# Expert stage in a fixed order, and neighborhood attention in 4 by 16 patches

## The chip, the cores and the metric

The kernel runs on one core of one Trainium2 chip. The metric is the time of one execution in microseconds of device time. The time before is the median of three runs; the profile is one execution taken by the hardware profiler.

## The reference

One encoder block on a sequence of 1024 tokens (16 rows of 64 columns) of width 1024, in float32:

```python
h = rms_norm(x, norm_mix_g)
(na_q, na_k, na_v, p_r, p_k, p_v, lat_w, lat_a, lat_g, mem_q, gates) = split_columns(h @ w_in)
y_na  = neighborhood_attention(na_q, na_k, na_v, na_rpb)      # 6 heads of 64
y_rw  = rwkv7_bidirectional(...)                              # 6 heads, two directions
y_mem = memory_attention(mem_q, rms_norm(mem), w_mem_kv)      # 4 heads, 256 memory rows
x = x + (sum of sigmoid(gate_b) * (y_b @ w_branch_b)) @ w_out
x = x + expert_choice_ffn(rms_norm(x), w_router, w_gate, w_up, w_down)
return rms_norm(x, norm_final_g)
```

Two parts matter here. In neighborhood attention the token at row r, column c sees 8 rows and 16 columns: the rows start at clip(r - 4, 0, 8), the columns at clip(c - 8, 0, 48), and each pair gets a bias `rpb[head, row offset, column offset]` before the softmax. In the expert stage each of 16 experts takes the 128 tokens with the highest affinity, and computes `silu(x Wg) * (x Wu)` (1024 to 2048) times `Wd` (2048 to 1024), scaled by the affinity and added to the tokens' rows.

## The kernel before

Every product in reduced precision is made from three: an operand is split into a hi part (rounded by a ScalarE copy) and a lo part (the rest, by a VectorE subtraction), and hi x hi, lo x hi and hi x lo are accumulated (`mm3`, lines 220 to 223).

The work goes by stages: input norms and projections; the RWKV scan with the other projections as filler; neighborhood attention, group norm and memory attention together; merge of the branches; output projection, router and top-k; experts; final norm. SP issues most loads and stores, in the order of its queue.

**Attention stage.** Head pairs j = 0, 1, 2 have 16 items each, one for a row r of 64 queries of two heads (128 partitions of scores), then 16 items of memory attention. `na_load(j)` loads k (`kt`), q, v (`VC`) and the bias table, splits k and q (`KT`, `qb`; q is masked per head), adds the column mask to the bias on GpSimd, and turns v into `VT` by 15 transposes, with one ScalarE copy for four of them. `na_item(j, r)` has eight parts: `score` (three matmuls of 512 key columns: 8 rows of 64, then bias and row maximum in one VectorE operation), `exp` (ScalarE), `recip` and `mul` (VectorE), `trans` (four transposes and a ScalarE copy), `mix` (value product, for four blocks of keys and two heads), `hi` and `lo` (result to `yh`, `yl`). The order is written out by hand: at slot n each part runs for the item that its lag in `PIPE` gives (score 0, exp 1, recip and mul 2, trans 3, mix 5, hi and lo 6). `na_load(0)` stands ahead of all items; `na_load(1)`, `na_load(2)` and `mem_load` begin at slots 1, 17 and 33, and group norm, one part per slot, at slot 5. Group norm loads its own data through SP and applies a tanh to `lg` on ScalarE at slot 6. Of `VC` and `kt` there is one buffer each.

**Expert stage.** The weights lie in 384 tiles of 1 MB, each loaded by SP into one of 14 buffers (`raw`, `RAWB`), and split by ScalarE into `ewh` (line 1212) and by VectorE into `ewl` (line 1213), of which there are four buffers each (`SPLB`). A step is one expert e and one block f of 512 of the 2048 hidden columns: two gate tiles (24 matmuls), the down part of the step before (24), two up tiles (24). The down part transposes the activation `sg` (line 1277), splits it into `ah` and `al` (lines 217 and 218) and multiplies by two down tiles (lines 1285 to 1287). `load_x` gathers an expert's 128 rows (line 1254), transposes and splits them; after an expert, `ye` is scaled and scattered with addition into `acc` (line 1292). The order of this stage is left to the framework's planner. At the end all rows of `acc` are normalised (line 1322) and stored while the last down part runs, and the last expert's rows are gathered, completed (line 1336), normalised and scattered over the stored ones.

Of the kernel before, what the change touches and what calls it, by code (L numbers as in the profile page):

```python
# [25 lines left out]
F32 = mybir.dt.float32  # L26
# [37 lines left out]
def shape_constants():  # L64
# [42 lines left out]
def lay(inputs):  # L107
# [36 lines left out]
    return {k: np.ascontiguousarray(v) for k, v in o.items()}  # L144


@with_exitstack
def block_kernel(ctx: ExitStack, tc: tile.TileContext, T, out, dbg=None, upto=99):
# [668 lines left out]
    def na_load(j):  # L817
        bias = ap.tile([128, 15, 64], F32, name="bias", bufs=2)
        q = ap.tile([128, S], F32, name="q", bufs=2)
        kt = ap.tile([128, S], F32, name="kt", bufs=1)  # L820
        VC = ap.tile([128, S], F32, name="VC", bufs=1)
        for t, src in ((kt, pna[3 + j]), (q, pna[j]), (VC, pna[6 + j]), (bias.rearrange("p r c -> p (r c)"), T["rpb"][:, j])):
            SP.dma_start(t, src)
        VT = ap.tile([128, 15, 128], F32, name="VT", bufs=2)
        qb = [ap.tile([128, 16, 2, 64], F32R, name=f"qb{v}", bufs=2) for v in "hl"]
# [7 lines left out]
        q = q.rearrange("p (r t) -> p r t", t=64)  # L833
        for h, r in ((0, 0), (1, 0), (0, 8), (1, 8)):
            hi, lo = (v[:, r:r + 8, h] for v in qb)
            V.tensor_scalar(hi, q[:, r:r + 8], C("hsel")[:, h:h + 1], None, op0=OP.mult)
            yield
            V.scalar_tensor_tensor(lo, q[:, r:r + 8], C("hsel")[:, h:h + 1], hi.bitcast(F32), op0=OP.mult, op1=OP.subtract)
            if r:
                yield  # L840
        G.tensor_tensor(bias, bias, C("nmask")[:, None, :].to_broadcast([128, 15, 64]), op=OP.add)
        for i0 in range(0, 15, 4):
            p = abank("tr")
            n = min(4, 15 - i0)
            for i in range(i0, i0 + n):
                t0 = i * 128 if i < 8 else (i - 8) * 128 + 64
                PE.transpose(p[:, (i - i0) * 128:(i - i0 + 1) * 128], VC[:, t0:t0 + 128], ident)
            A.activation(VT[:, i0:i0 + n], p[:, :n * 128].rearrange("p (i c) -> p i c", i=n), AF.Copy)
            yield

    def na_item(j, r):
        bias, KT, qb, VT = na[j]
        rs = min(max(r - 4, 0), 8)
        ro = rs - r + 7
        o = {}

        def score():
            s = abank("s")
            mm3(s, 0, 1, *(v[:, r].rearrange("p h t -> p (h t)") for v in qb), *(v[:, rs * 64:rs * 64 + 512] for v in KT))
            o["sb"] = sb = ap.tile([128, 512], F32, name="sb", bufs=4)  # L860
            o["st"] = st = ap.tile([128, 8], F32, name="st", bufs=4)
            V.tensor_tensor_reduce(out=sb, in0=s, in1=bias[:, ro:ro + 8, :].rearrange("p r c -> p (r c)"),
# [12 lines left out]
        def trans():  # L875
            p = abank("tr")
            for k in range(4):
                PE.transpose(p[:, k * 128:(k + 1) * 128], o["sb"][:, k * 128:(k + 1) * 128], ident)
            o["pt"] = ap.tile([128, 512], F32, name="pt", bufs=3)
            A.activation(o["pt"], p, AF.Copy)  # L880
# [486 lines left out]
```

## Time and profile before

| | |
|---|---|
| median of three runs | 2420.95 us (2419.74 to 2422.48) |
| profiled execution, first to last instruction | 2419.1 us |
| matmul queue (PE) busy | 2279.5 us, 94% |
| VectorE (DVE) busy | 1725.5 us, 71% |
| ScalarE (ACT) busy | 1334.0 us, 55% |
| GpSimd (POOL) busy | 592.8 us, 25% |
| moved by DMA | 588.55 MB, 243 GB/s in the mean |
| attention stage, about 823 to 999 us | 176 us |
| expert stage with the end, about 1250 to 2419 us | 1169 us |

How to read the lines: a row of the timeline is start in us, duration in us, engine, line of the kernel, instruction, the tile it writes and the tiles it reads, count, and in brackets the idle time of the engine before it with what ended it. PE is the matmul, PEld the weight load. A row of a stretch gives its length, then the busy time of PE, PEld, DVE, ACT and POOL with their instruction counts, the granted TensorE clock as a share of full speed, the busy share of the 16 DMA engines, and GB/s. A row of a group gives its busy time, the mean duration in ns, and idle time before. A row of the chain is start and duration of one piece. A row of the waits is who waited for whom: us in all, times, longest. Matmuls are pipelined, so starts tell their pace, not their durations.

### The profile page before, as it was taken

To read this page: it belongs to the slowest core of one execution; us is meant where nothing else is said; L and a number is where in the kernel's file an instruction comes from. 1 tells how busy PE (TensorE), PEld (TensorE's weight loads), DVE (VectorE), ACT (ScalarE), POOL (GpSimd) and SP (SyncE) were. 2 spreads that over 40 slices of the span, in tenths; PEclk is the share of its full clock that TensorE was granted. 3 is DMA by queue.
4 is the path that set the end of the run, shared out by engine and by line. 5 is a ranking of instruction groups with operands and counts; after the bars stand their busy time and mean duration, and the time that the engine had idled before them with its cause. 6 is when DMAs were issued, how large, how long until landed. Compare 5 with 4: busy or idle time off the path is not lost.

```text
span 2419.1 us, 34315 instructions
## 1 busy us (share of the span) xinstructions
PE 2279.5 (94%) x12931; PEld 1819.1 (75%) x12931; DVE 1725.5 (71%) x2155; ACT 1334.0 (55%) x1616; POOL 592.8 (25%) x1187
## 2 busy tenths in 40 slices
PE   7999999999999989999939999999999999999997
PEld 6677788877778767778727777777777777777775
DVE  6556556655665488762378888888888888888887
ACT  6554333333343378522236776776767667767675
POOL 1000666766666243340140000000011101011001
PEclk9999999999999999999969999999999999999998
DMA  6435443444343331363769999999999999999894
GB/s 233 151 137 209 129 122 98 117 126 125 98 119 96 122 111 64 116 191 121 250 267 372 357 367 364 355 360 375 362 370 362 361 359 374 365 375 367 295 413 173
DMA packets 193910, 588.55 MB, mean 243 GB/s; under 512 B 53072, under 2 KB 97360, under 8 KB 144592
## 3 DMA queue, kind: packets, MB, share of 16 engines
q1 hardware_dynamic: 187120, 562.88, 64.0%
q0 software_dynamic: 4752, 17.30, 2.8%
q10 hardware_dynamic: 1872, 6.17, 0.7%
q8 instruction: 102, 1.67, 0.3%
q14 instruction: 64, 0.52, 0.1%
HBM read 517.56 MB, written 68.73 MB: 242 GB/s over the span
## 4 chain that ended last, share of the span: by engine, by line
PE 64%; DVE 21%; issue 5%; ACT 4%; DMA 2%; POOL 2%; SPq 0%; POOLq 0%; DVEq 0%; ACTq 0%
PE acc L695 12%; DVE ewl L1213 8%; PE u L223 5%; PE y L1286 4%; PE y L1285 4%; PE y L1287 4%; PE u L221 3%; PE u L222 3%; PE acc L221 3%; PE acc L223 3%; PE acc L222 3%; PE g L221 3%; PE g L223 3%; PE g L222 3%; ACT ewh L1212 2%
## 5 line engine op out<-in xcount | busy, mean ns | idle before, releaser
L1213 DVE TENSOR_TENSOR ewl<-raw,ewh 128x2048 fp32r<-128x2048 f32 x380 | 861.7, 2289 | 162.0 <-ACT ewh L1212 161.8
L1212 ACT ACTIVATE ewh<-raw 128x2048 fp32r<-128x2048 f32 x384 | 732.2, 1917 | 289.0 <-PE y L1286 149.4
L223 PE MATMUL u<-ewl,xh 128*128 128x512 f32 x512 | 206.3, 403 | 23.8 <-DVE ewl L1213 22.0
L1292 POOL DMA_INDIRECT acc<-ye,idx x15 | 40.0, 2666 | 768.3 <-DVE ye L1291 768.3
L695 PE MATMUL acc<-hlo,wh 128*128 128x512 f32 x560 | 225.6, 403 | 0.0
L695 PE MATMUL acc<-hhi,wh 128*128 128x512 f32 x560 | 225.1, 402 | 0.0
L695 PE MATMUL acc<-hhi,wl 128*128 128x512 f32 x560 | 225.0, 402 | 0.0
L551 POOL TENSOR_TENSOR tmul<-tinv,blk 96x60 f32<-96x60 f32 (+24 forms) x496 | 172.1, 347 | 151.8 <-DMA blk<-ldr 114.3
L221 PE MATMUL u<-ewh,xh 128*128 128x512 f32 x512 | 205.5, 401 | 0.0
L1285 PE MATMUL y<-ewh,ah 128*128 128x512 f32 x512 | 194.7, 401 | 8.6 <-ACT ah L217 8.6
L221 PE MATMUL g<-ewh,xh 128*128 128x512 f32 x512 | 201.2, 393 | 0.0
L1286 PE MATMUL y<-ewh,al 128*128 128x512 f32 x512 | 200.4, 391 | 0.8 <-DVE al L218 0.8
L1287 PE MATMUL y<-ewl,ah 128*128 128x512 f32 x512 | 199.9, 390 | 0.0
L222 PE MATMUL u<-ewh,xl 128*128 128x512 f32 x512 | 199.9, 390 | 0.0
L223 PE MATMUL g<-ewl,xh 128*128 128x512 f32 x512 | 199.9, 390 | 0.0
L222 PE MATMUL g<-ewh,xl 128*128 128x512 f32 x512 | 199.5, 390 | 0.0
L553 POOL TENSOR_TENSOR tinv<-tinv,tmul 96x60 f32<-96x60 f32 (+24 forms) x496 | 176.2, 355 | 38.9
L223 PEld LDWEIGHTS u<-ewl,xh 128*128 128x128 f32 x512 | 96.0, 188 | 67.2 <-DVE ewl L1213 49.5
L1285 PEld LDWEIGHTS y<-ewh,ah 128*128 128x128 f32 x512 | 92.4, 189 | 42.3 <-ACT ah L217 23.7
L218 DVE TENSOR_TENSOR wl<-wraw,wh 128x1024 fp32r<-128x1024 f32 (+1 forms) x60 | 76.1, 1269 | 65.1 <-ACT wh L217 65.0
L695 PEld LDWEIGHTS acc<-hlo,wh 128*128 128x128 f32 x560 | 106.2, 190 | 20.6
L695 PEld LDWEIGHTS acc<-hhi,wl 128*128 128x128 f32 x560 | 105.9, 189 | 20.2
(309 smaller groups left out, 4409.4 us busy)
## 6 DMA issues: line engine op xcount, KB each, us to landing
raw<-in_wg_dram SPq DMA_DIRECT2D x128, 1024.0 KB
raw<-in_wu_dram SPq DMA_DIRECT2D x128, 1024.0 KB
raw<-in_wd_dram SPq DMA_DIRECT2D x128, 1024.0 KB
wraw<-in_wt_dram SPq DMA_DIRECT2D x46, 512.0 KB
pt<-pz SPq DMA_DIRECT2D x16, 768.0 KB
pgt<-po SPq DMA_DIRECT2D x48, 256.0 KB
gt<-pgt SPq DMA_DIRECT2D x16, 768.0 KB
blk<-ldr SPq DMA_DIRECT2D x64, 96.0 KB
```

The costliest lines, as they stand in the source:

```text
L218: V.tensor_sub(lo, src, hi.bitcast(F32))
L221: PE.matmul(out_, lh, rh, start=(k_ == 0), stop=False)
L222: PE.matmul(out_, ll, rh, start=False, stop=False)
L223: PE.matmul(out_, lh, rl, start=False, stop=(k_ == K - 1))
L551: G.tensor_tensor(tm[:, 0:m, 0:n], tt[:, 0:m, j:j + 1].to_broadcast([4 * NB, m, n]), lt[:, j, None, j + 1:32].to_broadcast([4 * NB, m, n]) ...
L553: G.tensor_tensor(tt[:, 0:m, j + 1:32], tt[:, 0:m, j + 1:32], tm[:, 0:m, 0:n], op=OP.add)
L695: PE.matmul(p, l[:, k], r[:, k, s0:s0 + 512], start=(k == 0 and i == 0), stop=(k == KD - 1 and i == 2))
L1212: A.activation(hi, raw, AF.Copy)
L1213: eng.tensor_tensor(lo, raw, hi.bitcast(F32), op=OP.subtract)
L1285: PE.matmul(o, ah[:, k], rh, start=(f == 0 and k == 0), stop=False)
L1286: PE.matmul(o, al[:, k], rh, start=False, stop=False)
L1287: PE.matmul(o, ah[:, k], rl, start=False, stop=(f == 3 and k == 3))
```

## The change

It has two parts.

In the expert stage the planner is replaced by an order written out by hand. The list `seq` holds the 384 tiles in the order of use (gate of step s, down of step s - 1, up of step s). Behind each tile's matmuls stand the hi copy of the tile that takes its buffer (`hi_of`) and the lo part of the one before that (`lo_of`), which in turn issues the load 14 tiles further on. The transposes of `sg` come between the two gate tiles of the next step; a tile's products with its hi part come before those with its lo part; the next expert's rows are transposed in two halves around the first up tile of block 2; half of `ye` is scaled on ScalarE. The loads of `acc` and some of the final norms move into the last steps.

In neighborhood attention an item is a patch of 4 rows by 16 columns in place of a row of 64. Its keys are the 8 or 12 rows and 24 or 32 columns that any of its queries can see, 192 to 384 in place of 512, in two or three blocks of four rows. The bias is laid out per kind of patch with the mask in it (9 kinds, 2240 columns for each head pair), so the mask addition goes. v is loaded as four column windows, and q is split per column group. Memory attention's k, v tiles share the buffers of `kt` and `VT`.

```diff
+NROW, NCOL = (8, 12, 8), (24, 32, 24)
+ROW0S, COL0S = (0, 0, 4, 8), (0, 8, 24, 40)
+RTYPE, CTYPE = (0, 1, 1, 2), (0, 1, 1, 2)
+NBIAS = int(BOFF[-1])
+WSUM = sum(NCOL[t] for t in CTYPE)
...
     def na_load(j):
-        bias = ap.tile([128, 15, 64], F32, name="bias", bufs=2)
+        bias = ap.tile([128, NBIAS], F32, name="bias", bufs=2)
-        VC = ap.tile([128, S], F32, name="VC", bufs=1)
-        for t, src in ((kt, pna[3 + j]), (q, pna[j]), (VC, pna[6 + j]), (bias.rearrange("p r c -> p (r c)"), T["rpb"][:, j])):
+        VC = ap.tile([128, 16 * WSUM], F32, name="VC", bufs=1)
+        for t, src in ((kt, pna[3 + j]), (q, pna[j]), (bias, T["rpb"][:, j])):
             SP.dma_start(t, src)
+        for c0, ct in zip(COL0S, CTYPE):
+            at, w = sum(v.shape[1] for v in VW), NCOL[ct]
+            VW.append(VC[:, at:at + 16 * w])
+            SP.dma_start(VW[-1].rearrange("p (r c) -> p r c", c=w), pna[6 + j].rearrange("p (r c) -> p r c", c=64)[:, :, c0:c0 + w])
...
-        G.tensor_tensor(bias, bias, C("nmask")[:, None, :].to_broadcast([128, 15, 64]), op=OP.add)
...
-    def na_item(j, r):
+    def na_item(j, g):
+        rg, cg = g // 4, g % 4
+        w, nc4 = NCOL[CTYPE[cg]], NROW[RTYPE[rg]] // 4
+        n = 4 * nc4 * w
...
         def trans():
-            for k in range(4):
-                PE.transpose(p[:, k * 128:(k + 1) * 128], o["sb"][:, k * 128:(k + 1) * 128], ident)
+            for k in range(nc4):
+                PE.transpose(p[:4 * w, k * 128:(k + 1) * 128], o["sb"][:, k * 4 * w:(k + 1) * 4 * w], ident)
...
+    with tc.tile_pool(name="eps", bufs=1, space=PSUM, reuse_waits="tile") as ps, tc.manual_schedule():
+        def hi_of(n):
+            if n < len(seq) and seq[n] not in his:
+                his[seq[n]] = hi = ep.tile([128, 2048], F32R, name="ewh", bufs=SPLB)
+                A.activation(hi, raws[seq[n]], AF.Copy)
+        def lo_of(n):
+            if n < len(seq) and seq[n] not in los:
+                los[seq[n]] = lo = ep.tile([128, 2048], F32R, name="ewl", bufs=SPLB)
+                V.tensor_sub(lo, raws.pop(seq[n]), his[seq[n]].bitcast(F32))
+            load(n + RAWB)
...
+        for s_ in range(steps + 1):
+            if s_ < steps:
+                gate_up(seq[at], pg)                      # first gate tile, at += 1
+            if s_:
+                PE.transpose(...)                         # sg of step s - 1, four blocks
+                split_to(*a, pt.rearrange("p (k t) -> p k t", k=4))
+            if s_ == steps:
+                finish(8 - len(stores))
+            if s_ < steps:
+                hi_of(at - 1 + SPLB)
+                lo_of(at - 2 + SPLB)
+                gate_up(seq[at], pg)                      # second gate tile
+                A.activation(sg, pg, AF.Silu)
+                hi_of(at - 1 + SPLB)
+                lo_of(at - 2 + SPLB)
+            if f == 1 and e + 1 < NE:
+                gather(e + 1)
+            if s_:
+                for b in range(2):
+                    down(seq[at], a, py)
+                    hi_of(at - 1 + SPLB)
+                    lo_of(at - 2 + SPLB)
+                if pf == 3 and pe + 1 < NE:
+                    scaled(pe, py)
+            if s_ >= steps - 2 and s_ < steps:
+                finish(s_ - steps + 3)
+            if f == 2 and e + 1 < NE:
+                x_half(e + 1, 0)
+            if s_ < steps:
+                gate_up(seq[at], pu)                      # first up tile
+                hi_of(at - 1 + SPLB)
+                lo_of(at - 2 + SPLB)
+                if s_ == steps - 1:
+                    finish(1)
+                if f == 2 and e + 1 < NE:
+                    x_half(e + 1, 1)
+                gate_up(seq[at], pu)                      # second up tile
+                V.tensor_mul(sg, sg, pu)
+                hi_of(at - 1 + SPLB)
+                lo_of(at - 2 + SPLB)
```

More of the change, by code (lines that the diff above doesn't have):

```diff
@@ L1245, in block_kernel, with load, gather @@
     mctx.close()
[L1248 removed]
+    steps = NE * 4
+    seq = []
+    for s_ in range(steps + 1):
+        if s_ < steps:
+            seq += [("wg", *divmod(s_, 4), b) for b in range(2)]
+        if s_:
+            seq += [("wd", *divmod(s_ - 1, 4), b) for b in range(2)]
+        if s_ < steps:
+            seq += [("wu", *divmod(s_, 4), b) for b in range(2)]
+    raws, his, los = {}, {}, {}
+    for k_ in seq[:RAWB]:
+        if k_ in first:
+            raws[k_] = first.pop(k_)
+    for k_, (hi, lo) in early.items():
+        his[k_], los[k_] = hi, lo
+    ts = []
+    with tc.tile_pool(name="eps", bufs=1, space=PSUM, reuse_waits="tile") as ps, tc.manual_schedule():
         def bank(tag, bufs):
             return ps.tile([128, 512], F32, name=tag, bufs=bufs)
[L1252 removed]
+        def load(n):
+            if n < len(seq):
+                if seq[n] not in raws and seq[n] not in his:
+                    raws[seq[n]] = fetch(*seq[n])
+            elif n - len(seq) < 8:
+                i = n - len(seq)
+                ts.append(rawt())
+                SP.dma_start(ts[i][:, 0:D], acc[i * 128:(i + 1) * 128, :])
+        def hi_of(n):
[7 more added lines that the diff above has]
+            load(n + RAWB)
+        def gather(e):
             xe = lv.tile([128, D], F32, name="xe")
@@ new lines, in down @@
+        def down(key, a, py):
+            _, e, f, b = key
+            ah, al = a
+            wh, wl = (v.pop(key).rearrange("p (a c) -> p a c", a=2) for v in (his, los))
+            for i, (l, r) in enumerate(((ah, wh), (al, wh), (ah, wl))):
+                for k in range(2):
+                    for n in range(2):
+                        PE.matmul(py[n], l[:, 2 * b + k], r[:, k, n * 512:(n + 1) * 512],
+                                  start=(f == 0 and b == 0 and i == 0 and k == 0), stop=(f == 3 and b == 1 and i == 2 and k == 1))
@@ new lines, in scaled, with gain @@
+        def scaled(e, py):
+            ye = lv.tile([128, D], F32, name="ye")
+            A.activation(ye[:, 0:512], py[0], AF.Copy, scale=tvT[:, e:e + 1])
+            V.tensor_scalar(ye[:, 512:D], py[1], tvT[:, e:e + 1], None, op0=OP.mult)
+            G.indirect_dma_start(out=acc[:, :], out_offset=bass.IndirectOffsetOnAxis(ap=idx[:, e:e + 1], axis=0),
+                                 in_=ye, in_offset=None, compute_op=OP.add)
+        def gain():
+            t = lv.tile([128, D], F32, name="xe")
+            A.dma_start(t, bass.AP(tensor=T["gfin"].tensor, offset=T["gfin"].offset, ap=[[0, 128], [1, D]]))
+            return t
```

217 lines of the change are left out of this document (106 added, 111 removed).

## The prediction

> **What bounds the kernel now.** I read the page's header and chain, then busy time by stage, then the matmul queue inside one step of each of the two changed stages, then the waits of the load queue.
>
> ```profile
> span 2419.1 us, 34315 instructions
> ...
> PE 64%; DVE 21%; issue 5%; ACT 4%; DMA 2%; POOL 2%; SPq 0%; POOLq 0%; DVEq 0%; ACTq 0%
> ...
> 823.00:999.00 176.00, 164.45 (x1580) 123.30 (x1579) 143.73 (x437) 128.57 (x350) 62.14 (x44) 1.00 0.29 97
> ```
>
> The chain of what ended last is 64% matmul and 21% VectorE. Neighborhood attention with group norm and memory attention takes 176 us (823 to 999), the matmul queue busy for 164 of them. Two tiles bound the expert stage: gate and up matmuls of the first and last weight tile.
>
> ```profile
> L223 PE MATMUL g<-ewl,xh x512: 389/389/560, 1252.9 to 2381.8; 128*128 128x512 f32 x171
> ...
> L223 PE MATMUL u<-ewl,xh x512: 387/389/506, 1258.3 to 2394.0; 128*128 128x512 f32 x171
> ```
>
> From 1252.9 to 2394.0 are 1141.1 us for 64 steps (16 experts, 4 blocks). One expert takes 71.64 us by two starts of the same hi copy:
>
> ```profile
> 1832.18 1.93 ACT ewh L1212
> ...
> 1903.82 1.93 ACT ewh L1212
> ```
>
> Inside one step, from the transposes of one activation (`tr`, line 1277) to the next:
>
> ```profile
> 1881.02 0.60 PE L1277 MATMUL tr<-cst,sg 128*128 128x128 f32 x4
> ...
> 1888.90 0.39 PE L223 MATMUL u<-ewl,xh 128*128 128x512 f32 x1
> ...
> 1898.42 0.39 PE L223 MATMUL g<-ewl,xh 128*128 128x512 f32 x1
> 1898.65 0.60 PE L1277 MATMUL tr<-cst,sg 128*128 128x128 f32 x4
> 1899.01 0.48 PE L221 MATMUL u<-ewh,xh 128*128 128x512 f32 x1
> 1899.33 0.39 PE L222 MATMUL u<-ewh,xl 128*128 128x512 f32 x1
> 1899.99 0.73 PE L1285 MATMUL y<-ewh,ah 128*128 128x512 f32 x2 [0.28 <-ACT ah L217]
> 1900.76 0.51 PE L223 MATMUL u<-ewl,xh 128*128 128x512 f32 x1
> ```
>
> The step is 1898.65 - 1881.02 = 17.63 us. From 1888.90 to 1898.42 lie 42 starts without a gap, so a 512-column matmul costs 9.52 / 42 = 0.2267 us, and a step's 72 cost 16.32. The four transposes cost 0.36, the first matmul behind them 0.09 more than usual: 16.77 of work, 0.86 lost. Most of it stands after the transposes: 1899.33 to 1900.76 is 1.43 us for three matmuls (0.68), since only two up matmuls separate the transposes from the down matmul that needs `ah`.
>
> ```profile
> 1881.21 0.60 ACT L1303 ACTIVATE sg<-g 128x512 f32<-128x512 f32 x1 [1.03 <-PE g L223]
> 1881.71 0.59 ACT L217 ACTIVATE ah<-tr 128x512 fp32r<-128x512 f32 x1
> ...
> 1875.77 0.69 DVE L1309 TENSOR_TENSOR sg<-sg,u 128x512 f32<-128x512 f32 x1 [0.28 <-PE u L223]
> 1876.38 6.69 DVE L1213 TENSOR_TENSOR ewl<-raw,ewh 128x2048 fp32r<-128x2048 f32 x3
> ```
>
> ScalarE makes `sg` at 1881.21, and only then `ah` at 1881.71, done near 1882.3. VectorE is next in load: three lo subtractions in 6.69, so 2.23 each, and 0.61 from one 512-column operation to the next start.
>
> **The change part by part: experts.** It removes no matmul there. What moves is order: the transposes of `sg` go between the two halves of the gate, so 12 matmuls (2.72 us) run while `ah` and `al` are made; each weight tile's hi part is used in its first eight matmuls, so its buffer comes free four matmuls earlier; hi and lo are issued right behind the tile whose buffers they take, four tiles ahead. The cost of a step should be the 16.77 of work. The next expert's eight transposes, now two groups of four, add 2 x 0.45 per expert, as both kinds of switch do above. The first step has no down part (-5.44 - 0.45). Sum: 64 x 16.77 - 5.9 + 15 x 0.9 = 1080.9, and 1080.2 between the two starts that I measured 1141.1 by: 60.9 us of possible gain. I take 58, leaving 3 us for single late tiles.
>
> This needs covers. VectorE: six lo (13.4), two 0.61 operations, and per expert two halves of `xl` and one of `ye` (the other half goes to ScalarE), at 0.61 to 0.74 each: about 15.1 of 17.0 us per step. In the fixed order it waits twice a step: for `ah` (transposes at 2.7, `ah` at 3.8; the lo before it ends at 3.0, so 0.8 lost) and for the last up matmul before `sg`; behind the first stand `al`, wanted at 6.8, and lo parts wanted a whole tile later. So 15.9 of 17.0, and the lead of four tiles covers the jitter. ScalarE: six hi of 1.93 with three or four of 0.6 fit in 17. The load queue:
>
> ```profile
> 1832.20:1903.80 71.60, 70.11 (x313) 55.81 (x312) 61.34 (x37) 50.43 (x34) 6.45 (x2) 1.00 0.98 368
> ...
> 2296.00:2340.00 44.00, 43.38 (x192) 34.67 (x192) 36.09 (x22) 30.46 (x20) 0.34 (x1) 1.00 1.01 420
> ...
> SPq L1070 <- DVE ewl L1213: 951.0, 361, 24.5
> ...
> ACT ewh L1212 <- DMA raw<-in_wd_dram: 0.8, 1, 0.8
> ```
>
> Loads wait for the lo part that frees their buffer (951 us), and a hi waited only once for a load (0.8 us). One expert moved 368 GB/s x 71.6 us = 26.35 MB; at 68 us that is 388 GB/s, and 420 was reached where loads had piled up. The cover is thin: with gathers and scatters between, the 0.98 share stood at 368. [...]
>
> At the start the four early tiles and the gather of expert 0 are as before. Gathers (POOL), scatters (POOL) and the `gfin` load (ScalarE's queue) keep their count, some a step earlier; nothing on their queues waits behind them. On SP the eight loads of `acc` stand behind the last weight tile, so no weight is late for them; they wait for expert 14's scatter, a step earlier. The end:
>
> ```profile
> 2396.10 0.68 DVE L1309 TENSOR_TENSOR sg<-sg,u 128x512 f32<-128x512 f32 x1
> ...
> 2408.24 1.40 DVE L1336 SCALAR_TENSOR_TENSOR raw<-y,tvT,raw 128x512 f32<-128x512 f32 x2
> ```
>
> The last `sg` product now starts 1.7 us after its up matmul (2394.0 + 0.39), behind final norms; it will start at once, and four norms remain behind it where now seven do. They still hold the path to 2408.24's operation, one at a time through POOL's power: I take -2 (0 to -4).
>
> **Neighborhood attention.** One item of the 48 now:
>
> ```profile
> 885.24 0.48 PE L221 MATMUL s<-KTh,qbh 128*128 128x512 f32 x1
> ...
> 886.01 0.60 PE L878 MATMUL tr<-cst,sb 128*128 128x128 f32 x4
> 886.54 0.69 PE L887 MATMUL av<-pt,VT 128*64 128x64 f32 x16
> 887.15 0.50 PE L221 MATMUL s<-KTh,qbh 128*128 128x512 f32 x1
> ```
>
> 1.91 us: 0.77 score, 0.53 transposes, 0.61 for sixteen value matmuls. A patch has 192, 256, 288 or 384 window columns, 12 patches each, mean 280 instead of 512.
>
> ```profile
> 25.81 0.28 PE L222 MATMUL acc<-mhi,wl 128*128 128x256 f32 x1
> ...
> 27.71 0.28 PE L223 MATMUL acc<-mlo,wh 128*128 128x256 f32 x1
> ...
> 840.60:957.00 116.40, 107.60 (x1111) 80.58 (x1110) 99.51 (x311) 87.42 (x223) 49.14 (x35) 1.00 0.31 107
> ...
> L873 DVE TENSOR_SCALAR sb<-sb,st 128x512 f32<-128x512 f32 x48 | 36.0, 750 | 0.1
> ...
> L862 DVE CUSTOM_DVE_ANT_0 sb<-s,bias 128x512 f32<-128x512 f32 x48 | 32.7, 682 | 0.1
> ```
>
> At 256 columns a matmul costs 1.90 / 16 = 0.119 us, so at 280 about 0.129: three save 0.29. 1.5 transposes fewer save 0.14 (at 0.09 each), six of sixteen value matmuls 0.23. So 0.66 x 48 = 32 of the matmul queue's 107.6 us in these 116.4. VectorE had 99.5. Its two wide operations shrink by 0.31 and 0.34 if in proportion, by nothing if fixed; I take 0.24 and 0.15, since the multiply also waits for POOL. That is 19 us less, 1.5 more for eight small q pieces in place of four, so VectorE at 82 becomes the bound. At the 92% by which the queue filled the stretch now, 89 us: 27 saved (18 to 33). POOL loses three mask additions, off the path.
>
> What it adds is the load of V. Each head pair's `VC` was 128 rows of 4 KB; it becomes four column windows with 128 x 16 pieces of 96 or 128 bytes each, 8192 pieces. `bias` grows from 0.49 to 1.15 MB and goes ahead of them. Rows of such pieces, from 285.45 to 287.12 us and 251.5 to 254.2:
>
> ```profile
> DMA packets 1000, 0.44 MB, mean 265 GB/s; under 512 B 858, under 2 KB 858, under 8 KB 1000
> ...
> DMA packets 927, 0.49 MB, mean 181 GB/s; under 512 B 32, under 2 KB 914, under 8 KB 926
> ```
>
> The first is 858 packets of 128 bytes in 1.67 us, 1.95 ns each (16 us for 8192); the second, mostly 512 bytes, 2.9 ns (24 us). I take 17, as the first is nearest in size. The old 0.5 MB at 420 GB/s takes 1.2.
>
> ```profile
> 833.53 4.81 DMA VC<-pna
> ...
> 842.64 0.69 DVE L862 CUSTOM_DVE_ANT_0 sb<-s,bias 128x512 f32<-128x512 f32 x1
> ...
> 854.32 1.04 ACT L780 ACTIVATE lg<-lg 128x1024 f32<-128x1024 f32 x1
> ```
>
> The first pair is not hidden: its `VT` transposes stand in the matmul queue ahead of all items. `VC` landed at 838.3; now 15.8 later, and 2.7 for `bias` ahead of it, then 2.1 for transposes and copies as now: the first score reduction at about 859.8 instead of 842.64, +17. The second pair's `VC` follows once the first's buffer is free (857), and group norm's first loads queue behind it on SP. Item slot 6 puts the tanh of `lg` into ScalarE's queue, 11.7 us after the first reduction now; `lg` will land near 877, the slot comes near 870, and every exponential stands behind it: +6.5 (0 to 12). The third pair's pieces arrive one by one, 9 slots ahead: 0 (0 to 7). Sum -27 + 17 + 6.5 = -3.5, bounds -18 to +25. Memory attention, merge and router keep their work.
>
> Sum: 2419.1 - 58 - 2 - 3.5 = 2355.6 of span. The profiled span stands 1.9 below the median of 2420.95, so 2357.5; I predict 2358.
>
> **Rivals.** The transfers become the bound (0.12): if share 1.0 in this mix is 368 / 0.98 = 376 GB/s, an expert takes 70.1 us, the gain is 16 x 1.55 = 25, and the time 2391. For it: 0.98. Against: 420 at the burst and the one late load. [...]
>
> VectorE keeps the bound (0.08):
>
> ```profile
> DVE ewl L1213 <- ACT ewh L1212: 161.8, 186, 4.4
> ```
>
> 161.8 us over 64 steps is 2.5 per step; added to 15.1 it gives 17.6, today's step. If the fixed order leaves these waits in place, only the attention part and the end remain: 2415. Against: hi parts now come two tiles before their lo.
>
> The attention gains without stalls (0.12): if loads come as early as the buffers allow and group norm's `lg` isn't behind them, -20 instead of -3.5: 2341.
>
> The other side (0.05): the pieces are dear. Three loads, each with a wait behind it, cost x - 17 more each; the 63 us of gain are gone at x = 38 us, 4.6 ns a piece, 1.6 times the slowest row above. At twice that row, 48 us, the time is 2451. The place is 834 to 882 us and the same before items 9 and 26. Against: both rows.
>
> **How the numbers follow.** The likeliest case has 0.63, its own range 2340 to 2378. Low end 2336: the attention at its best with the whole 61 of the experts. High end 2393: the transfer rival. Within 0.2% is 4.8 us, what a measurement of this kernel can tell from no change: 0.02, from the VectorE rival's middle. Slower by more: 0.05 + 0.01. Faster: 0.92.
>
> **What would show it.** Steps of 16.8 to 17.0 us between groups of `sg` transposes, no wait of `y` for `ah`, and waits of `ewl` for `ewh` below 30 us in all. The first score reduction near 860 with the transposes of `VC` waiting for a load from 838, and a wait of ScalarE's tanh for `lg`. 48 items in 89 us with VectorE at 90%. Wrong if hi parts wait for `raw` again and again, if steps stay above 17.3, or if the first reduction comes later than 870.

## The result: 2366.2 us, 2.3% faster

The changed kernel takes 2366.19 us (median of 4 runs, 2361.88 to 2367.32) against 2420.68 (2419.74 to 2422.48): ratio 0.9767, 95% interval 0.9756 to 0.9779. I predicted 2358 and 2336 to 2393. The total is inside, but of the terms behind it two were wrong by 10 us or more, in opposite directions, and one had the wrong sign.

First the page's header, its chain, and the busy times of the attention stage (columns: PE, weight loads, VectorE, ScalarE, GpSimd, granted clock, DMA share, GB/s) of the changed kernel:

```profile
span 2364.1 us, 33731 instructions
...
PE 80%; DVE 11%; ACT 3%; DMA 2%; issue 2%; POOL 1%; SPq 1%; POOLq 0%; ACTq 0%; DVEq 0%
...
823.00:999.00 176.00, 150.08 (x1245) 111.61 (x1245) 130.65 (x464) 113.45 (x354) 55.01 (x41) 0.90 0.43 116
```

The chain is now 80% matmul (64% before) and 11% VectorE (21%). The attention stage looks worse: the matmul queue is busy for 150 of 176 us, and its granted clock is 0.90 where it was 1.00.

**The expert stage.** The new lines: 1328 and 1329 multiply the hi part of a weight tile, 1331 its lo part, 1340 the down tiles, 1388 transposes `sg`, 1300 makes hi, 1305 lo. From the timeline of the matmul queue:

```profile
1251.99 0.63 PE L1328 MATMUL g<-ewh,xh 128*128 128x512 f32 x1
...
1879.76 0.60 PE L1388 MATMUL tr<-cst,sg 128*128 128x128 f32 x4
1880.11 0.48 PE L1328 MATMUL g<-ewh,xh 128*128 128x512 f32 x1
...
1896.54 0.60 PE L1388 MATMUL tr<-cst,sg 128*128 128x128 f32 x4
```

the list of one tile (its last two times are the first and the last start):

```profile
L1331 PE MATMUL u<-ewl,xh x512: 388/389/395, 1260.1 to 2336.0; 128*128 128x512 f32 x171
```

the waits (us in all, times, longest), and the busy times in the 71.60 us of one expert before:

```profile
DVE ewl L1305 <- ACT ewh L1300: 6.5, 2, 4.6
...
ACT ewh L1300 <- DMA raw<-in_wu_dram: 0.7, 1, 0.7
...
PE y L1340 <- ACT ah L233: 0.7, 1, 0.7
```

```profile
1832.20:1903.80 71.60, 71.60 (x329) 59.26 (x328) 63.76 (x38) 54.49 (x38) 5.54 (x2) 1.00 0.99 388
```

From the third gate matmul (1251.99) to the last up matmul (2336.02) are 1084.0 us, 1141.1 before. The step between two groups of transposes is 1896.54 - 1879.76 = 16.78 us, and no matmul in it waits. Of the 63 steps between such groups 47 take 16.78 to 16.81 us, the 15 with the next expert's transposes 17.76, and the last 19.95. VectorE's 161.8 us of waits for hi parts are 6.5; `y` waited for `ah` once, behind the last step. In the same 71.60 us the core moved 388 GB/s, where it had moved 368, at a DMA share of 0.99.

**The end.** VectorE's queue behind the last up matmul:

```profile
2335.99 1.29 DVE L1359 SCALAR_TENSOR_TENSOR raw<-raw,ss,xe 128x1024 f32<-128x1024 f32 x1 [0.66 <-POOL ss L213]
2337.20 2.28 DVE L1305 TENSOR_TENSOR ewl<-raw,ewh 128x2048 fp32r<-128x2048 f32 x1
2339.40 0.14 DVE L212 TENSOR_SCALAR rinv_t<-ss 128x1 f32<-128x1 f32 x1
2340.21 1.28 DVE L1359 SCALAR_TENSOR_TENSOR raw<-raw,ss,xe 128x1024 f32<-128x1024 f32 x1 [0.66 <-POOL ss L213]
2341.41 0.68 DVE L1436 TENSOR_TENSOR sg<-sg,u 128x512 f32<-128x512 f32 x1
```

The last `sg` product (line 1436) starts at 2341.41, 5.4 us after the last up matmul's start; before, it was 2.1 us (2396.10 - 2394.00). Ahead of it stand the product of one norm, the last lo part and a whole second norm with its wait for GpSimd's root. From the last up matmul to the end it takes 28.10 us, 25.05 before.

**Neighborhood attention.** Line 866 transposes `VC`, 886 is the score reduction, 897 the multiply, 858 and 859 make hi and lo of `q`. From the timelines of the matmul queue, the load queue, VectorE and ScalarE:

```profile
839.31 0.39 PE L711 MATMUL acc<-hlo,wh 128*128 128x512 f32 x1
843.17 1.06 PE L866 MATMUL tr<-cst,VC 128*96 128x128 f32 x4 [3.47 <-DMA VC<-pna]
...
850.22 7.02 SPq L844 DMA_DIRECT2D VC<-pna  x4
...
859.05 0.43 SPq L775 DMA_DIRECT2D lg<-plat  x1
...
850.92 0.36 DVE L886 CUSTOM_DVE_ANT_0 sb<-s,bias 128x192 f32<-128x192 f32 x1 [6.92 <-ACT VT L867]
...
863.44 1.06 ACT L796 ACTIVATE lg<-lg 128x1024 f32<-128x1024 f32 x1 [3.50 <-DMA lg<-plat]
...
892.91 0.63 ACT L851 ACTIVATE KTh<-kt 128x512 fp32r<-128x512 f32 x1 [3.20 <-DMA kt<-pna]
```

the DMA packets of 7.94 us (840.01 to 847.95), and the busy times of item slots 0 to 27 and 28 to 47, whose bounds are score reductions:

```profile
DMA packets 8444, 1.38 MB, mean 174 GB/s; under 512 B 8286, under 2 KB 8286, under 8 KB 8427
```

```profile
850.90:920.40 69.50, 54.71 (x444) 40.40 (x443) 54.26 (x200) 41.16 (x127) 22.99 (x18) 0.82 0.63 172
920.40:956.50 36.10, 34.28 (x359) 25.86 (x358) 29.66 (x129) 29.70 (x97) 20.11 (x15) 1.00 0.16 52
```

The same two stretches before:

```profile
842.60:912.50 69.90, 61.49 (x617) 45.20 (x618) 60.47 (x186) 50.02 (x127) 27.79 (x20) 1.00 0.40 140
912.50:957.50 45.00, 45.00 (x501) 34.80 (x499) 37.53 (x128) 37.01 (x95) 20.42 (x15) 1.00 0.14 46
```

The first score reduction comes 11.6 us after the last projection matmul (839.31), 5.1 before. From the reduction of slot 28 (920.4) to that of slot 47 (956.0) an item takes 35.6 / 19 = 1.87 us; before (912.5 to 956.5) 44.0 / 19 = 2.32. But slots 0 to 27 take 69.5 us, and took 69.9: nothing was gained there, although VectorE is busy for 54.3 us and was for 60.5.

All landmarks in one table, in us: from the last projection matmul to the first score reduction ("start"), from there to the first score of memory attention ("items"), from the third gate matmul to the last up matmul ("experts"), from that to the end, and the median time.

| kernel | start | items | experts | end | median |
|---|---|---|---|---|---|
| before | 5.1 | 114.8 | 1141.1 | 25.1 | 2420.7 |
| changed | 11.6 | 105.6 | 1084.0 | 28.1 | 2366.2 |
| e1_experts | 5.8 | 114.9 | 1083.4 | 28.1 | 2367.1 |
| e2_attention | 12.4 | 106.7 | 1141.3 | 25.1 | 2418.3 |
| e12_late_transposes | 11.6 | 106.9 | 1145.8 | 28.0 | 2425.2 |
| e4_product | 11.5 | 107.1 | 1083.2 | 25.7 | 2359.8 |
| e7_tail | 11.6 | 108.6 | 1083.3 | 25.0 | 2361.3 |
| e3_vc_whole | 5.5 | 105.0 | 1084.3 | 28.1 | 2358.2 |
| e9_no_adds | 11.5 | 100.8 | 1082.9 | 29.1 | 2355.7 |
| e5_early_loads | 5.4 | 96.7 | 1083.8 | 28.1 | 2344.7 |
| e6_hi_scalar | 9.5 | 96.8 | 1084.2 | 28.1 | 2349.9 |
| e8_all | 8.9 | 94.1 | 1083.9 | 25.2 | 2346.5 |
| e10_best | 5.4 | 96.4 | 1083.8 | 24.3 | 2339.4 |
| e11_spread | 5.5 | 91.7 | 1083.3 | 24.1 | 2338.3 |

Two spreads limit what can be read. The stages ahead of attention are the same code everywhere, and ended between 834.8 and 839.3 us in these profiles, and the medians come from four sessions, in which the kernel before took 2420.7 (changed), 2421.4 (e1 to e4), 2423.0 (e5 to e8) and 2421.7 (e9 to e12); so small differences are read from intervals, not totals. And the items of the five kernels that have the changed kernel's attention (changed, e2, e4, e7, e12) took 105.6 to 108.6.

### The profile page after: what moved, and what is told of

It is laid out like the page before. It is cut to its first block, busy times and chain, and to the rows that moved or that the text cites. A ratio compares the mean times of both kernels' runs of the same rounds, so it can differ in the third digit from the quotient of the medians.

```text
span 2364.1 us, 33731 instructions
## 1 busy us (share of the span) xinstructions
PE 2236.5 (95%) x12574; PEld 1813.1 (77%) x12574; DVE 1693.5 (72%) x2164; ACT 1322.4 (56%) x1631; POOL 595.0 (25%) x1184
## 4 chain that ended last, share of the span: by engine, by line
PE 80%; DVE 11%; ACT 3%; DMA 2%; issue 2%; POOL 1%; SPq 1%; POOLq 0%; ACTq 0%; DVEq 0%
PE y L1340 14%; PE acc L711 14%; PE g L1328 5%; PE g L1329 5%; PE g L1331 5%; PE u L1328 5%; PE u L1329 5%; PE u L1331 5%; PE acc L237 3%; PE acc L238 3%; PE acc L239 3%; PE tr L1388 1%; DVE Gst L656 1%; DVE rsl L234 1%; POOL m L1074 1%
## 5 line engine op out<-in xcount | busy, mean ns | idle before, releaser
L1305 DVE TENSOR_TENSOR ewl<-raw,ewh 128x2048 fp32r<-128x2048 f32 x380 | 849.8, 2284 | 6.5 <-ACT ewh L1300 6.5
L1300 ACT ACTIVATE ewh<-raw 128x2048 fp32r<-128x2048 f32 x380 | 720.8, 1914 | 113.7 <-PE u L1329 85.4
L1328 PE MATMUL g<-ewh,xh 128*128 128x512 f32 x512 | 206.6, 403 | 0.0
L1340 PE MATMUL y<-ewh,ah 128*128 128x512 f32 x512 | 137.9, 391 | 0.7 <-ACT ah L233 0.7
L1331 PE MATMUL g<-ewl,xh 128*128 128x512 f32 x512 | 137.5, 390 | 0.0
L1340 PE MATMUL y<-ewh,al 128*128 128x512 f32 x512 | 137.4, 390 | 0.0
L1331 PE MATMUL u<-ewl,xh 128*128 128x512 f32 x512 | 137.0, 389 | 0.0
L1340 PE MATMUL y<-ewl,ah 128*128 128x512 f32 x512 | 136.9, 389 | 0.0
L711 PEld LDWEIGHTS acc<-hhi,wh 128*128 128x128 f32 x560 | 106.6, 190 | 20.3
L233 ACT ACTIVATE ah<-tr 128x512 fp32r<-128x512 f32 x64 | 38.4, 599 | 143.6 <-PE tr L1388 143.6
```

What stands on the lines that cost most here:

```text
L711: PE.matmul(p, l[:, k], r[:, k, s0:s0 + 512], start=(k == 0 and i == 0), stop=(k == KD - 1 and i == 2))
L1300: A.activation(hi, raws[seq[n]], AF.Copy)
L1305: V.tensor_sub(lo, raws.pop(seq[n]), his[seq[n]].bitcast(F32))
L1328: PE.matmul(p, xh[:, 4 * b + k], wh[:, k], start=(b == 0 and k == 0), stop=False)
L1331: PE.matmul(p, xh[:, 4 * b + k], wl[:, k], start=False, stop=(b == 1 and k == 3))
L1340: PE.matmul(py[n], l[:, 2 * b + k], r[:, k, n * 512:(n + 1) * 512], start=(f == 0 and b == 0 and i == 0 and k == 0), stop=(f == 3 and b == ...
```

## Experiments

### Do the parts add up? (e1_experts, e2_attention)

Each is the kernel before with one of the two parts of the diff: e1_experts with everything from `early` on, e2_attention with `window_bias` and its table, `na_load`, `na_item` and `mem_load`.

> The kernel before with the fixed order of the expert stage alone; attention as before. Theory (the parts add up): the expert stage runs at 16.8 us per step, 57 us shorter between its first and last weight matmul, and the time from the last up matmul to the end is 3 us longer than before, as in the changed kernel; 2420.7 - 54 = 2366.5 us (2365 to 2368). The stage before attention ends at 837.5 as before. Rival (the 1.8 us by which the stage before attention ended later in the changed kernel, 839.3 for 837.5, belong to the new expert code): 2368.5, and it ends at 839.3 here too. Rival (without the new attention the loads of the first weights come at another time, so the expert gain is another): the stage differs from 1084.0 us by more than 2.

> The kernel before with the attention in patches alone; experts as before. Theory (two opposite terms that nearly cancel): the first score reduction comes 6.5 us later after the last projection matmul than before, the 48 items then take 10 us less, so the stage is 3.5 us shorter, 2420.7 - 3.5 = 2417 us if the stage before ends as before, 2419 if the patches delay it by the 1.8 us seen. Rival (the attention's small gain is spoilt only together with the new expert part): 2400 to 2410.

They add up within the noise: 54.3 us less with the experts alone (ratio 0.9775, 0.9759 to 0.9791), 3.1 with the attention alone (0.9985, 0.9975 to 0.9994), 57.4 together, and 54.5 with both at once. The difference of 2.9 is less than the 3.9 on either side that the first interval leaves. The stage ahead ended at 837.7 in the first, 837.2 in the second: the 1.8 us of the changed kernel's profile belong to neither part. The loss at the end (28.1) comes with the experts, the late start and the shorter items with the attention.

### What carries the expert gain? (e12_late_transposes)

```diff
-            if s_:
-                pt = bank("tr", 2)
...
-                split_to(*a, pt.rearrange("p (k t) -> p k t", k=4))
             if s_ < steps:
...
                 gate_up(seq[at], pg)
...
-                sg = ep.tile([128, 512], F32, name="sg", bufs=2)
+                old, sg = sg, ep.tile([128, 512], F32, name="sg", bufs=2)
                 A.activation(sg, pg, AF.Silu)
+                if s_:
+                    a = halves(old)
```

`halves` holds the lines taken out: the four transposes, `ah` and `al`. They now stand behind the second gate tile, with only the next `sg` ahead of them on ScalarE, and the down tiles follow at once.

> The changed kernel with the transposes of sg, ah and al moved behind the second gate tile and the next sg, right ahead of the down matmuls: that part of the fixed order undone and even tightened, all else kept. Theory A (the gain of the expert stage is the cover of 12 matmuls for ah): the down matmul waits for sg, transposes and ah, 1.1 to 1.4 us per step, so the stage is 64 x 1.1 to 1.4 = 70 to 90 us longer than 1084 and the kernel slower than before, 2430 to 2455. Theory B (the gain came from the weight tiles, hi and lo in time): 10 to 30 us longer, 2376 to 2396.

The stage takes 1145.8 us, 61.8 more, and the kernel 2425.2 (ratio 1.0016, 1.0006 to 1.0026): undoing this one placement gives back the whole gain of the stage. Theory A's mechanism, at a smaller size than its 70. Its matmul queue and its waits:

```profile
1895.69 0.60 PE L1372 MATMUL tr<-cst,sg 128*128 128x128 f32 x4
1897.03 1.19 PE L1340 MATMUL y<-ewh,ah 128*128 128x512 f32 x4 [0.74 <-ACT ah L233]
```

```profile
PE y L1340 <- ACT ah L233: 46.5, 63, 0.7
```

From the transposes to the first down matmul are 1.34 us where the next gate matmul came after 0.35, so 0.99 per step; 0.74 of it is the wait for `ah`. I had expected 1.1 to 1.4. The early hi and lo parts, still in place here, save nothing by themselves that this run shows. No run has the early transposes in the planner's order, so whether they would have been enough alone stays open.

### Why is the end longer? (e4_product, e7_tail)

```diff
                 hi_of(at - 1 + SPLB)
-                lo_of(at - 2 + SPLB)
-                if s_ == steps - 1:
-                    finish(1)
+                if s_ < steps - 1:
+                    lo_of(at - 2 + SPLB)
...
                 V.tensor_mul(sg, sg, pu)
+                if s_ == steps - 1:
+                    lo_of(at - 3 + SPLB)
```

> The changed kernel with one of the final norms and the last lo part moved behind the last sg product in VectorE's queue. Theory A (the 3 us lost behind the last up matmul are the lateness of that product, 2341.4 for an up part that ends near 2336.4): the product starts 4 us earlier and the end comes 3 to 4 us earlier, 2362 to 2363. Theory B (as predicted: the norms hold the path, one at a time through POOL's power): the product starts 4 us earlier, the five norms left behind it take 2.1 us each and the end moves by less than 1.5 us, 2365 to 2367.

The product starts 1.2 us after the last up matmul, 4.2 earlier, and the end comes 2.4 earlier: between the theories, and both have a part. (The time, 2359.8, lies below both, as the stages ahead of attention ended 3.3 us earlier in its profile.) VectorE's queue shows who holds the rest:

```profile
2333.48 0.68 DVE L1435 TENSOR_TENSOR sg<-sg,u 128x512 f32<-128x512 f32 x1
...
2336.88 0.14 DVE L212 TENSOR_SCALAR rinv_t<-ss 128x1 f32<-128x1 f32 x1
2337.68 1.28 DVE L1359 SCALAR_TENSOR_TENSOR raw<-raw,ss,xe 128x1024 f32<-128x1024 f32 x1 [0.66 <-POOL ss L213]
...
2347.19 1.40 DVE L1443 SCALAR_TENSOR_TENSOR raw<-y,tvT,raw 128x512 f32<-128x512 f32 x2
```

Five norms of 2.07 us each, root and product in turn, run from 2336.88 to 2347.19, when the sum for the last expert may start. So e7_tail does the norms in two groups (two, then three), each with one root for all its rows, and puts the products of the group of three behind that sum:

```diff
+        def squares(tt):
...
+            for i, t in enumerate(tt):
+                A.activation(t[:, D:], t[:, 0:D], AF.Square, accum_out=ss[:, i:i + 1])
+            rinv_of(ss[:, 0:len(tt)], ss[:, 4:4 + len(tt)], len(tt), 1.0 / D, 1e-6)
...
-                finish(8 - len(stores))
+                ss = squares(ts[3:5])
+                for i in range(2):
+                    store(3 + i, ss, i)
+                ssb = squares(ts[5:8])
```

> The changed kernel with the last sg product ahead as in the kernel before in this list, and the five norms left behind it done in two groups: the squares of a group first, one reciprocal root for all its rows, then the products, three of them behind the last expert's sum. Theory (after the product the norms hold the path, 2.07 us each of which 1.28 are VectorE's): from the last up matmul to the end 21 to 22.5 us, in place of 28.1 in the changed kernel and 25.7 with the product alone; 2359 to 2360. Rival (the last stores or the last scatter hold the end): 24.5 to 25.7.

The sum now starts 10.5 us after the last up matmul (14.9 with the product alone, 17.3 in the changed kernel), yet the end is only 0.6 us earlier: the rival was right.

```profile
2348.42 3.67 DVE L1377 SCALAR_TENSOR_TENSOR raw<-raw,ssb,xe 128x1024 f32<-128x1024 f32 x3
...
2354.73 1.04 POOL L1465 DMA_INDIRECT out_dram<-raw,idx  x1 [4.62 <-issue]
```

The last product ends at 2352.09, and the scatter starts at 2354.73; in e4_product the scatter followed the last product by 0.3 us. The code lets it wait for all eight stores. By the trace the packets of the last store end at 2353.30, 1.43 us ahead of the scatter; in e4_product they had ended at 2349.57, 2.5 us before the last product did. e10_best and e11_spread, below, repeat the distance: 2332.79 and 2334.23, 2330.50 and 2331.94. So it is the last store that holds the scatter here.

### The pieces of V (e3_vc_whole)

```diff
-        for t, src in ((kt, pna[3 + j]), (q, pna[j]), (bias, T["rpb"][:, j])):
+        for t, src in ((kt, pna[3 + j]), (q, pna[j]), (VR, pna[6 + j]), (bias, T["rpb"][:, j])):
             SP.dma_start(t, src)
-        VW = []
...
+        def cut(cg):
+            w = NCOL[CTYPE[cg]]
+            cuts.append(ap.tile([128, 512], F32, name="VC", bufs=2)[:, :16 * w])
+            A.activation(cuts[cg].rearrange("p (r c) -> p r c", c=w),
+                         VR.rearrange("p (r c) -> p r c", c=64)[:, :, COL0S[cg]:COL0S[cg] + w], AF.Copy)
```

> The changed kernel with V loaded as 128 rows of 4 KB by one transfer per head pair and cut into the four windows on ScalarE (12 copies of 384 or 512 columns, some 0.6 us each), in place of four transfers in pieces of 96 and 128 bytes. Theory A (the pieces cost the attention most of its gain, at the start and in the load queue, whose issues of VC took up to 8 us): the first score reduction comes 6 us earlier (5.5 instead of 11.6 us after the last projection matmul), the wait of the tanh for lg (3.5 us) goes, and the time falls by 8 to 12 us, to 2354 to 2358. Theory B (after the first pair another engine bounds the items, VectorE with its quarter q pieces next to POOL): what the start gains is kept, nothing more; -5 to -6, 2360. Theory C (the 12 copies on ScalarE cost what the pieces cost): 2364 to 2368.

Theory B. The start takes 5.5 us, 6.1 less, and the tanh no longer waits for `lg` (of the 8.0 us in the medians the rest lies outside these intervals); the items take 105.0 and slots 0 to 27 the same 69.5 as with the pieces. The ratio is 0.9739 (0.9722 to 0.9755). So the pieces cost the start, and were not what held the items.

### What holds slots 0 to 27? (e5_early_loads, e6_hi_scalar, e9_no_adds)

e5 and e6 start from e3_vc_whole, with one of these edits each:

```diff
-        side = {1: na_load(1), 17: na_load(2), 33: mem_load()}
+        side = {1: na_load(1), 14: na_load(2), 33: mem_load()}
```

```diff
-                V.tensor_scalar(hi, qg, C("hsel")[:, h:h + 1], None, op0=OP.mult)
+                A.activation(hi, qg, AF.Copy, scale=C("hsel")[:, h:h + 1])
```

> The kernel with V in one transfer, and the loads and preparation of the third head pair three item slots earlier (slot 14, not 17), ahead of a load of group norm that waits for GpSimd. In the kernel with V in one transfer the first copy of that pair's K waits 3.1 us for its load and the step between two score reductions there is 5.49 us. Theory A (that wait is on the path): the items (first score reduction to first memory score, 105.0 us) take 102, the time falls by 3 to 2355. Theory B (VectorE, with the quarter q pieces of that pair in the same slots, takes the place of the wait): 104 to 105, the time stays within 1 us of 2358.

> The kernel with V in one transfer, and the hi part of each quarter q piece made on ScalarE, not VectorE (24 pieces; in the items VectorE spends 9.1 us on the hi parts of pairs 2 and 3 and 10.5 on the lo parts). Theory A (VectorE's queue is what holds the items wherever q pieces stand in it, slots 6 to 27): the items take 105.0 - 6 to 9 = 96 to 99 us, and the time falls to 2349 to 2352. Theory B (the waits for loads and the hand-overs between engines hold them): 103 to 105 us, 2356 to 2358. Theory C (ScalarE, busy 70% there, becomes the bound): 105 to 108.

e9 starts from the changed kernel and leaves out three of group norm's additions on GpSimd, so it no longer computes the same block:

```diff
-            G.tensor_tensor(y0, y0, y1, op=OP.add)
-            G.tensor_tensor(b0, b0, b1, op=OP.add)
-            G.tensor_tensor(y1, y1, b0, op=OP.add)
```

> The changed kernel without three of group norm's additions on GpSimd per tile (the sums of the two directions' y, of their b, and y + b: left out, their inputs are still loaded). In the items GpSimd is busy 43 of 105.5 us; these additions are about half of that, and VectorE's operations take longer beside GpSimd (hi parts of q 0.34 us at the least, 1.36 at the most). Theory A (the items are slow where q pieces stand in the queue because VectorE shares something with GpSimd): the items take 92 to 98 us. Theory B (late loads, of lg and of the third pair's K, and the hand-overs behind them hold those slots): 101 to 105 us.

e5's items take 96.7 us, 8.3 less, more than the 3 that theory A gave (its time, 2344.7, is 13.5 below e3's, and the rest lies outside the items); slots 0 to 27 fall from 69.5 to 61.6 with the same work in them:

```profile
841.80:911.30 69.50, 54.63 (x455) 40.32 (x453) 54.85 (x200) 44.22 (x136) 23.43 (x18) 0.83 0.47 166
```

and with the third pair earlier:

```profile
840.70:902.30 61.60, 54.10 (x454) 40.37 (x452) 51.65 (x201) 45.83 (x138) 23.14 (x18) 0.86 0.46 165
```

VectorE's busy time there fell by 3.2 us and its idle time by 4.7 (from 14.7 to 10.0). The move shifts the loads and the q pieces together, so it does not tell the wait for K from what the pieces meet in the slots they stand in. e6's items take 96.8, 8.2 less, theory A; but the hi parts of the first pair now stand on ScalarE ahead of everything, and the start is 4.1 longer. So two different moves each win back 8 us, and together (e8, below) 10.9: they cure the same slots. e9 gives 100.8, 4.8 less than the changed kernel and 6 to 8 less than the other kernels with its attention: between the two theories, just below B, so the additions are a part of the loss and not all of it. They also stand in group norm's own chain, so the run does not show by which way they cost it. A hi part of `q` (line 855 there) took 396 ns, 590 in the changed kernel's slots 0 to 27 (the rows with its 9.4 us further down):

```profile
L855 DVE TENSOR_SCALAR qbh<-q,cst 128x256 fp32r<-128x256 f32 x16 | 6.3, 396 | 0.0
```

How VectorE and GpSimd meet is seen in the changed kernel, in slot 24; GpSimd's timeline, VectorE's, and the matmul queue that waits:

```profile
907.62 1.27 POOL L829 TENSOR_TENSOR yl<-y,yh 128x512 fp32r<-128x512 f32 x1 [3.88 <-ACT yh L828]
908.85 1.32 POOL L793 TENSOR_TENSOR y<-y,y 128x512 f32<-128x512 f32 x1
910.12 1.44 POOL L794 TENSOR_TENSOR b<-b,b 128x512 f32<-128x512 f32 x1
...
905.41 0.34 DVE L858 TENSOR_SCALAR qbh<-q,cst 128x256 fp32r<-128x256 f32 x1
...
907.88 1.16 DVE L858 TENSOR_SCALAR qbh<-q,cst 128x256 fp32r<-128x256 f32 x1
909.07 1.37 DVE L859 SCALAR_TENSOR_TENSOR qbl<-q,cst,qbh 128x256 fp32r<-128x256 f32 x1
910.37 1.35 DVE L858 TENSOR_SCALAR qbh<-q,cst 128x256 fp32r<-128x256 f32 x1
911.75 0.48 DVE L859 SCALAR_TENSOR_TENSOR qbl<-q,cst,qbh 128x256 fp32r<-128x256 f32 x1
...
912.86 0.84 PE L902 MATMUL tr<-cst,sb 128*96 128x128 f32 x3 [3.57 <-DVE sb L897]
```

The hi piece at 905.41 takes 0.34 us and the lo piece at 911.75, with GpSimd idle, 0.48; the three between take 1.16 to 1.37, and each ends 0.15 to 0.3 us after the GpSimd operation that ran when it began (907.62 + 1.27 = 908.89, and 907.88 + 1.16 = 909.04; 910.17 and 910.44; 911.56 and 911.72). By what mechanism, no run shows. Behind the four pieces stands the multiply for which the transposes at 912.86 waited 3.57 us.

### Together (e8_all, e10_best, e11_spread)

e8_all is e5, e6 and e7_tail in one. e10_best keeps the hi parts of the first pair on VectorE, and orders the last norms so that the root of the next precedes the product of the one before:

```diff
-                V.tensor_scalar(hi, qg, C("hsel")[:, h:h + 1], None, op0=OP.mult)
+                if j:
+                    A.activation(hi, qg, AF.Copy, scale=C("hsel")[:, h:h + 1])
+                else:
+                    V.tensor_scalar(hi, qg, C("hsel")[:, h:h + 1], None, op0=OP.mult)
...
+                for i in (3, 4, 5, 6):
+                    nq[i] = square(ts[i])
+                    root(nq[i])
+                    if i > 3:
+                        store(i - 1, nq[i - 1])
```

e11_spread adds to e10 one q pair per slot:

```diff
                 V.scalar_tensor_tensor(lo, qg, C("hsel")[:, h:h + 1], hi.bitcast(F32), op0=OP.mult, op1=OP.subtract)
-                if cg % 2 or not h:
-                    yield
+                yield
```

> All of it together: V in one transfer, hi parts of q on ScalarE, the third pair's loads three slots earlier, the last product ahead and norms in groups. If the parts add up: items 94 to 98 us, end 21 to 22.5 us after the last up matmul, 2342 to 2347. If the attention part is held by something else once VectorE is relieved: 2350 to 2354.

> V in one transfer; the third pair three slots earlier; hi parts of q on ScalarE for the second and third pair alone; the last product ahead, and the norms behind it one by one but with the next one's root ahead of the product of the one before, the last store some 3 us earlier. Theory: first reduction 5.4 us after the last projection matmul (9.5 with all hi parts on ScalarE), items 94 to 96, end 22 to 23 us after the last up matmul in place of 25.0 to 25.7, as the last scatter waits for the last store: 2337 to 2341 us. Rival for the end (the last expert's own chain, sum, square, root, product, holds it): 24.5 to 25. Rival for the items (the 3 us that hi parts on ScalarE seemed to save came from the later start alone): 96.7.

> As the one before, with one q piece pair per item slot, eight slots, in place of six slots of which two hold two pairs. Theory (VectorE's bursts hold the items): the items take 1 to 3 us less than in the kernel before in this list. Rival (the waits have already gone): the same within 0.5 us.

e8: 2346.5 (ratio 0.9685, 0.9669 to 0.9702), items 94.1, end 25.2. That is inside the 2342 to 2347, but the parts do not add up: it is no faster than e5 alone (2344.7). Its items are 2.7 us shorter and its end 2.9, but its start is 3.5 longer, and from the first memory score to the third gate matmul, in code that is the same, it took 2.3 longer in its profile. e10: 2339.4 (0.9659, 0.9646 to 0.9672). Its start is 5.4 as expected. Its items take 96.4, as the rival had it: beside the earlier loads the hi parts on ScalarE bring nothing that this run shows, and e8's 94.1 went with its start, 3.5 us later. The end took 24.3, neither the 22 to 23 of the theory nor the rival's 24.5; the last store still holds the scatter, which starts 2.5 us behind the last product. e11's items take 91.7, 4.7 less, more than the theory's 1 to 3; its time, 2338.3 (0.9662, 0.9649 to 0.9675), can't be told from e10's, as the stages behind attention took 1.9 us longer in its profile. e10 and e11 beat both kernels, the changed one by 27 to 28 us.

One companion of all these moves is separated by no run: the granted clock of TensorE. In slots 0 to 27 it was 1.00 before, 0.82 in the changed kernel, 0.83 in e3, 0.86 in e5 and e9, 0.90 in e6, 0.81 in e10 and 0.97 in e11. First those slots and one stretch of them in e10, then the slots in e11:

```profile
840.40:901.80 61.40, 56.39 (x451) 42.94 (x449) 45.89 (x184) 50.98 (x154) 22.86 (x18) 0.81 0.46 164
...
875.60:889.30 13.70, 13.70 (x79) 10.85 (x78) 9.14 (x39) 9.72 (x31) 3.30 (x3) 0.50 0.22 83
```

```profile
841.60:898.50 56.90, 48.05 (x460) 36.56 (x458) 46.41 (x184) 50.21 (x154) 23.78 (x18) 0.97 0.55 192
```

For 13.7 us of e10 the matmul queue is busy throughout at half clock, and VectorE for 9.1. So what e11 wins over e10 can be the clock as well as the bursts, and what the hi parts on ScalarE are worth beside the earlier loads is hidden by e10's lower clock. That the bursts hold the items is not shown.

## Why the prediction came out right

**Against the profiled execution** I summed -58 - 2 - 3.5 = -63.5; the span fell by 55.0. The landmarks close it: experts -57.1, end +3.05, attention -3.6 (last projection matmul to first merge matmul, 162.75 to 159.19), and +1.8 ahead of attention and +0.9 between merge and experts, where the code is the same.

**Experts: right, in size and reason.** 57.1 for 58; steps of 16.78 for 16.77; VectorE busy 63.76 of 71.60 us, 14.9 per step, for 15.1 to 15.9; waits for hi parts 6.5 for "below 30". e12 shows that the cover of 12 matmuls for `ah` carries it. The transfer rival falls with its 376 GB/s: 388 were moved, and a hi part waited for a load once (0.7 us). The VectorE rival falls with its 161.8.

**The end: wrong sign.** The step that failed is "it will start at once": I counted the norms behind the product and not the ones that the fixed order puts ahead of it. -2 became +3.05, and e4 gives back 2.4. That the norms "still hold the path" was right once the product was early.

**Attention: right by two misses.** The sum -3.5 was measured as -3.6, by other terms:
- Start, +17: +6.5. The mis-sized term is the piece, taken at 1.95 ns. 8286 small packets in 7.94 us are 0.96 ns each; the row I took the price from, 858 packets in 1.67 us, was half as fast. (The terms given, 838.3 + 15.8 + 2.7 + 2.1, make 858.9, not 859.8, and the lower bound of -18 for the sum does not follow from -33 + 17.)
- The tanh's wait for `lg`, +6.5 (0 to 12): 3.5.
- Items with the stalls inside them, -27 + 6.5 + 0 = -20.5: -9.3. (Memory attention adds -0.8.) The pace of 89 / 48 = 1.85 us is what slots 28 to 47 do (1.87), and VectorE's work came out as summed (54.3 + 29.7 = 84 for 82). (The multiply that "also waits for POOL": before, between 840 and 960 us, 17 of 47 took 0.66 to 1.91 us, each beside a GpSimd operation, and the 30 others 0.47 to 0.52. Its mean fell from 750 to 563 ns, 0.19 us for the 0.15 I took.) But the agreement of the pace is luck: in those slots VectorE, which I had as the bound at 90%, is busy 29.66 of 36.10 us (82%), and the matmul queue 34.28 (95%). What failed is "at the 92% by which the queue filled the stretch now": VectorE is busy 54.3 of 69.5 us, 78%, in slots 0 to 27. The matmul queue, which I had counted at full clock, had 0.82 there: in slices of 0.8 us it stands at 1.00 or 0.50 but where it changes, so (1 - 0.82) x 2 x 69.5 = 25 of the 69.5 us were at half clock. The eight small q pieces were priced at 1.5 us of VectorE; lo and hi took 8.6 + 4.8 us in those slots before and take 10.2 + 9.4 now:

```profile
L838 DVE SCALAR_TENSOR_TENSOR qbl<-q,cst,qbh 128x512 fp32r<-128x512 f32 x9 | 8.6, 955 | 0.0
L836 DVE TENSOR_SCALAR qbh<-q,cst 128x512 fp32r<-128x512 f32 x8 | 4.8, 602 | 0.0
```

```profile
L859 DVE SCALAR_TENSOR_TENSOR qbl<-q,cst,qbh 128x256 fp32r<-128x256 f32 x16 | 10.2, 637 | 0.6
L858 DVE TENSOR_SCALAR qbh<-q,cst 128x256 fp32r<-128x256 f32 x16 | 9.4, 590 | 0.0
```

And the third pair, "0 (0 to 7)", cost a wait of 3.2 us for its K, and with the q pieces that e5 moves along with it the 8 us that e5 wins.

So the rival "the attention gains without stalls" (-20) was right about what was there to be had: e11 has it, with 5.5 of start and 91.7 of items. The rival of dear pieces was wrong by the price itself.

## What to carry to other kernels

In a fixed order an operation that stands ahead of the path can cost time as one behind it does (in e4_product the last `sg` product came 4.2 us earlier and the end 2.4): go through the whole queue of the engine up to the operation that ends last, not only what follows it. A pace worked out from a sum of busy times was met here where the queue holds only that work (1.87 us an item for 1.85 in slots 28 to 47, and by luck), and missed in slots 0 to 27 (69.5 / 28 = 2.48); where preparation for the next round is woven in, look at what it waits for and which engine it meets, slot by slot. Read the granted clock beside the busy share of a stretch: a queue that looks full can be full of matmuls at half clock, as for 13.7 us of e10_best. And a total that fits proves no term: check each with its own landmark.

## What the hardware showed that I had not expected

- The DMA share stood at 0.98 for 368 GB/s and at 0.99 for 388 with the same pieces: a share near 1 did not mean that the rate was at its limit.
- Four loads of 2048 pieces each took SP's queue 7.02 us from 850.22 (the twelve of the kernel 0.53 to 8.01 each, 1.40 in the median), where `lg`, 128 rows, took 0.43 at 859.05 and was issued only behind them.
- The mean clock of TensorE fell while the kernel became faster (0.975 for 0.984 over the whole). Around the first wait:

```profile
841.80:852.00 10.20, 6.11 (x25) 4.79 (x26) 3.07 (x12) 2.74 (x5) 0.00 (x0) 0.50 1.16 246
852.00:855.40 3.40, 2.04 (x14) 1.49 (x13) 3.12 (x13) 2.79 (x10) 1.76 (x2) 1.00 0.96 263
855.40:862.20 6.80, 6.52 (x40) 4.46 (x39) 6.52 (x24) 2.81 (x10) 0.80 (x1) 0.50 1.20 191
```

The clock was 0.50 from inside the gap between the last projection matmul (839.31) and the first transposes of `VC` (843.17, 3.47 us of wait), full from 852.0, and 0.50 again from 855.4. At 0.50 the second of two 256-column matmuls started 0.21 us behind the first (850.84 and 851.05), at 1.00 0.12 (954.08 and 954.20). Between 848.60 and the return at 852.0 the queue was busy for 3.18 of 3.40 us. The first fall came when the wait was some 2 us old (839.70 to 841.8), the second after 3.4 us in which the queue was busy for 2.04 and no wait was longer than 1.05; and in e10_best the clock stayed at 0.50 for 13.7 us with the queue busy throughout (shown above). What sets the clock is not shown by these rows, and what its falls cost was not measured by itself.
